# Up projection of a conv-gated FFN: activations as the stationary operand, 512 weight columns moving, and the result turned by transposing DMAs

## The chip, the cores and the metric

The kernel runs on one core of one Trainium2 chip. The metric is the device time of one launch in microseconds (us), the median over runs of the same program. A difference of 0.2%, some 4 us here, is about what such a measurement can tell from no change.

## The reference

Two layers of a bidirectional encoder trunk work on 256 tokens of width 2048 (float32). In each layer a normed copy of `x` goes through one combined input projection, a windowed attention and a spatial gating unit, and an output projection back into `x`. Then comes the feed-forward part, the only part that the change touches in what it computes from what:

```
def rms_norm(x, g):
    y = xf * lax.rsqrt(jnp.mean(xf * xf, axis=-1, keepdims=True) + EPS)
    return y * g

def conv_gated_ffn(h, w_up, conv_w, conv_b, w_down):
    a = depthwise_conv_centred(h @ w_up, conv_w, conv_b)   # 3 taps along the 256 tokens
    g, u = jnp.split(a, 2, axis=-1)                        # 5632 gate, 5632 up columns
    return (jax.nn.silu(g) * u) @ w_down

x = x + conv_gated_ffn(rms_norm(x, norm2_g[l]), w_up[l], conv_w[l], conv_b[l], w_down[l])
```

`w_up` is 2048 x 11264 per layer, `w_down` 5632 x 2048. The depthwise convolution takes, for each channel, the neighbours of a token, so it wants channels on the partitions and tokens along the free dimension.

## The kernel before, in words

**Precision.** Every product of float32 matrices is made of three products in the matmul's 32-bit replicated format `F32R`: each operand is split into a rounded part `hi` and a rest `lo`, and hi·hi, hi·lo and lo·hi are added in PSUM. For weights, ACT makes `hi` from a loaded 1 MB block `raw` (L128), and DVE makes `lo` as `raw - hi` (L112). `raw` has three buffers, `hi` and `lo` four tiles of 128 x 1024 each; one block fills two tiles of each. Activations are split once and kept: 16 tiles `acts[k]` of 128 x 2 x 256, channel k·128.. on the partitions, part 0 rounded, part 1 the rest.

**Two forms of product.** `rows_by_cols` (L161 to L186) serves the input projection, the output projection and the down projection. It holds a 128 x 128 piece of the activations in the array and moves 512 weight columns past it: for each of four k in a block and each half m of the tokens it issues two matmuls with `hi` and one with `lo` as the moving side (L168), 24 matmuls per 1 MB block. The result has tokens on the partitions. `pair` (L222 to L243) and `opening` (L246 to L276) serve the up projection the other way round: a 128 x 128 piece of the weight is held, and the activations move. With `hi` held, both parts of the activation move as 512 columns (L234, in `opening` L275); with `lo` held, only part 0, 256 columns (L240, in `opening` L270). One call of `pair` makes 256 gate channels and the 256 up channels that belong to them in two PSUM tiles: 64 matmuls of 512 columns and 64 of 256, out of 4 MB of weights. The result has channels on the partitions, as the convolution wants it.

**Up stage.** 5632 channels are 44 groups of 128. The first half of the stage makes groups 0 to 23 (12 pairs, the first by `opening`), then the down projection multiplies these; the second half makes groups 24 to 43 (10 pairs), and the down projection takes those. Per layer that is up (12 pairs), down (4 column blocks of 6 weight blocks), up (10 pairs), down (4 column blocks of 5). After each pair, `joined` (L278) adds the two halves of the PSUM tile (ACT copies one, L281; DVE adds, L283), L833 multiplies by the norm factor, which `as_rows` (L363) has spread over the partitions with two PE transposes, `convolved` runs the three taps (ACT L837, DVE L838 and L841), ACT applies SiLU (L855), DVE multiplies gate and up (L857), and `split_plain` splits the product for the down projection (L296, L297).

**Turning rows into columns.** Where a result of `rows_by_cols` is needed with channels on the partitions, the kernel already has a way: ACT copies float32 words apart into their low and high 16-bit halves (L422 in the attention, L575 in `next_rows`), SP issues transposing DMAs on the halves (L429, L582), and ACT puts the halves together again (`together`, L435, and L589 in `next_rows`).

**Order.** A scheduler decides the order on each engine from the order in the program and from priorities; each engine then runs its own list strictly in that order, with waits on the others. `urgent()` raises the priority of what stands in it. `waiting` is a list of steps; `let_in`, called in the middle of each weight block of `rows_by_cols`, issues the steps that stand there, so that the parts of a chain come one weight block after the other. All weight loads and all transposing DMAs are issued by SP and use one queue.

Of the kernel before, what the change touches and what calls it, by code (L numbers as in the profile page):

```python
# [8 lines left out]
F32 = mybir.dt.float32  # L9
# [6 lines left out]
P = 128  # L16
# [11 lines left out]
W = 512  # L28
# [14 lines left out]
def encoder(ctx: ExitStack, tc: tile.TileContext, xT, x, w_in, w_gu, w_o, w_up, w_down, wsT, pcol, prow, rope, out):  # L43
# [4 lines left out]
    slots = pool("slots", 43)  # L48
    rowp = pool("rowp", 4)
# [12 lines left out]
    def row(tag):  # L62
        return rowp.tile([P, W], F32, tag=tag, name=tag)
# [157 lines left out]

    def pair(acts, ws):  # L222
        pss, his, los, later = [mm(), mm()], [], [], []
        for n, w in enumerate(ws):
            hs = []
            for b in range(0, len(acts), UB):
                h, lo = split_weights(w[:, b * UW : (b + UB) * UW], later=later if n else None)
                hs += h
                los += lo if n == 0 else []
            for k in range(len(acts)):  # L230
                for i in range(2):
                    c = k % KB * UW + i * P
                    x1 = acts[k].rearrange("p a b -> p (a b)")
                    nc.tensor.matmul(pss[n][:, i, :], hs[k // KB][:, c : c + P], x1, start=k == 0, stop=False)  # L234
        for n in range(2):
            los = split_later(later) if n else los
            for k in range(len(acts)):
                for i in range(2):
                    c = k % KB * UW + i * P
                    nc.tensor.matmul(  # L240
                        pss[n][:, i, :SEQ], los[k // KB][:, c : c + P], acts[k][:, 0, :], start=False, stop=k == len(acts) - 1
                    )
        return pss  # L243


    def opening(acts, ws, last_step):  # L246
        pss = [mm(), mm()]
        for b0, b1 in ((0, 2), (2, 3), (3, 4)):
            w0, w1 = b0 * KB * UW, b1 * KB * UW
            if b1 - b0 == 2:  # L250
                tiles = [split_weights(w[:, w0:w1]) for w in ws]
            else:
                with urgent():
                    raw = rawp.tile([P, 4 * W], F32, tag="raw", name="raw")
                    for n, w in enumerate(ws):
# [686 lines left out]
```

## Time and profile before

| | us |
|---|---|
| median of 3 runs | 1992.83 (1992.35 to 1993.45) |
| span of the profiled execution, first to last instruction | 1990.9 |
| what lies around the span (median less span) | 1.9 |
| TensorE (PE) busy in the span | 1985.5 |
| VectorE (DVE) busy | 1367.6 |
| ScalarE (ACT) busy | 1134.5 |
| up stage, layer 0: first half, second half | 267.91 to 534.68, 665.27 to 887.31 |
| up stage, layer 1: first half, second half | 1258.22 to 1524.99, 1655.58 to 1878.46 |

The profile is of one execution. A row of a group gives the line, the engine, the operation, output and input names, the count, the busy time of the group, the mean duration of one, and the idle time of the engine ahead of it. Matmuls are pipelined, so the mean duration of one (390 ns) is longer than the distance from one to the next; the distance is read from the chain of work that ended last, which lists stretches of instructions with start, length and count. Busy shares over the whole span mix stages; the tables by stretch of time give them for one stage.

### The profile page before, as it was taken

Reading aid. Unit: us, or ns where it says so; the run is one execution under the profiler, and the core shown is the slowest. Engines: PE = TensorE matmul, PEld = TensorE weight load, DVE = VectorE, ACT = ScalarE, POOL = GpSimd, SP = SyncE. Lnnn points to the kernel's source line nnn. Section 1 sums busy time; section 2 is a strip of 40 time slices with the busy share of each in tenths; the row PEclk is TensorE's granted clock in tenths of the full one; section 3 lists DMA queues with packets and bytes.
Section 4 is the critical chain, followed back from the end, with each engine's and each line's share of the span. In section 5 each row is a group of like instructions: output and inputs, shape, how many; then the busy total and the mean of one; then the engine's idle time right before and its main releaser. Section 6 shows DMA issues by size and latency. Waiting matters only on the chain.

```text
span 1990.9 us, 26332 instructions
## 1 busy us (share of the span) xinstructions
PE 1985.5 (100%) x10292; PEld 1704.8 (86%) x10292; DVE 1367.6 (69%) x1930; ACT 1134.5 (57%) x1514; POOL 23.3 (1%) x25
## 2 busy tenths in 40 slices
PE   9999999999999999999999999999999999999999
PEld 8888888888888888888888888888888888888887
DVE  6778677777754577775566786777777445777753
ACT  6786585556543455556667675855555344555542
POOL 0100000000000000000000000000000000000000
PEclk9999999999999999999999999999999999999999
DMA  9754674455555544556767536745545554455563
GB/s 341 243 161 149 219 222 169 170 208 207 198 191 192 188 170 174 212 207 204 219 205 237 161 142 226 198 169 206 207 180 211 191 192 167 171 208 203 201 212 127
DMA packets 95580, 391.15 MB, mean 196 GB/s; under 512 B 43744, under 2 KB 45024, under 8 KB 50912
## 3 DMA queue, kind: packets, MB, share of 16 engines
q1 hardware_dynamic: 94736, 388.74, 56.6%
q8 instruction: 80, 1.31, 0.3%
q10 hardware_dynamic: 720, 0.73, 0.1%
q14 instruction: 44, 0.36, 0.1%
HBM read 378.43 MB, written 2.10 MB: 191 GB/s over the span
## 4 chain that ended last, share of the span: by engine, by line
PE 97%; ACT 1%; DVE 1%; DMA 1%; issue 0%; SPq 0%; POOL 0%; DVEq 0%; ACTq 0%
PE mm L168 42%; PE mm L234 31%; PE mm L240 16%; PE mm L209 2%; PE mm L275 1%; PE tp L168 1%; PE mm L214 1%; PE mm L270 1%; PE tp L308 0%; PE tp L751 0%; PE tp L310 0%; DVE lo L112 0%; PE tp L309 0%; DMA raw<-in_w_up 0%; ACT hi L128 0%
## 5 line engine op out<-in xcount | busy, mean ns | idle before, releaser
L112 DVE TENSOR_TENSOR lo<-raw,hi 128x1024 fp32r<-128x1024 f32 (+1 forms) x708 | 839.4, 1215 | 417.4 <-ACT hi L128 277.1
L128 ACT ACTIVATE hi<-raw 128x1024 fp32r<-128x1024 f32 (+1 forms) x708 | 730.3, 1050 | 606.8 <-PE mm L168 330.9
L168 PE MATMUL mm<-hi,sl 128*128 128x512 f32 x2480 | 667.6, 390 | 0.1
L234 PE MATMUL mm<-sl,hi 128*128 128x512 f32 x2688 | 617.8, 389 | 0.2 <-ACT hi L128 0.2
L234 PEld LDWEIGHTS mm<-sl,hi 128*128 128x128 f32 x2688 | 501.9, 188 | 103.5 <-ACT hi L128 1.1
L168 PEld LDWEIGHTS mm<-hi,sl 128*128 128x128 f32 x2480 | 464.5, 188 | 97.2 <-DVE sl L289 0.9
L168 PE MATMUL mm<-lo,sl 128*128 128x512 f32 x1240 | 382.6, 390 | 0.0
L240 PEld LDWEIGHTS mm<-sl,lo 128*128 128x128 f32 x2688 | 328.1, 192 | 3.3
L240 PE MATMUL mm<-sl,lo 128*128 128x256 f32 x2688 | 329.1, 283 | 0.0
L168 PEld LDWEIGHTS mm<-lo,sl 128*128 128x128 f32 x1240 | 232.5, 188 | 47.9
L838 DVE SCALAR_TENSOR_TENSOR sc<-ev,pc,sc 128x255 f32<-128x255 f32 x176 | 80.6, 481 | 94.0 <-ACT sc L837 94.0
L281 ACT COPY ev<-mm 128x512 f32<-128x512 f32 x96 | 55.4, 577 | 122.5 <-PE mm L240 114.8
L837 ACT ACTIVATE sc<-ev,pc 128x256 f32<-128x256 f32 x176 | 99.1, 589 | 0.0
L841 DVE SCALAR_TENSOR_TENSOR sc<-ev,pc,sc 128x255 f32<-128x255 f32 x176 | 80.6, 481 | 2.9
L296 ACT ACTIVATE sl<-sl 128x256 fp32r<-128x256 f32 x88 | 31.8, 409 | 72.8 <-DVE sl L857 72.8
L283 DVE TENSOR_TENSOR ev<-mm,ev 128x512 f32<-128x512 f32 x96 | 65.6, 683 | 0.0
L209 PE MATMUL mm<-sl,hi 128*128 128x512 f32 x256 | 61.6, 391 | 0.0
L833 DVE TENSOR_TENSOR ev<-ev,rb 128x512 f32<-128x512 f32 x88 | 60.1, 682 | 0.1
L209 PEld LDWEIGHTS mm<-sl,hi 128*128 128x128 f32 x256 | 47.3, 188 | 9.2
L289 DVE SCALAR_TENSOR_TENSOR sl<-sl,pc 128x256 fp32r<-128x256 f32 x96 | 42.6, 479 | 17.7 <-ACT sl L288 17.6
L297 DVE TENSOR_TENSOR sl<-sl 128x256 fp32r<-128x256 f32 x88 | 33.5, 422 | 19.4 <-ACT sl L296 19.4
L288 ACT ACTIVATE sl<-sl,pc 128x256 fp32r<-128x256 f32 x96 | 43.2, 497 | 1.1 <-DMA sl<-in_xT 0.9
(124 smaller groups left out, 813.2 us busy)
## 6 DMA issues: line engine op xcount, KB each, us to landing
raw<-in_w_up SPq DMA_DIRECT2D x172, 1024.0 KB, 5.2
raw<-in_w_down SPq DMA_DIRECT2D x88, 1024.0 KB, 4.9
raw<-in_w_in SPq DMA_DIRECT2D x38, 1024.0 KB, 5.1
raw<-in_w_o SPq DMA_DIRECT2D x32, 1024.0 KB, 4.9
raw<-in_w_gu SPq DMA_DIRECT2D x16, 1024.0 KB, 4.9
raw<-in_w_up SPq DMA_DIRECT2D x8, 512.0 KB, 4.5
sl<-in_prow SPq DMA_DIRECT2D x12, 256.0 KB, 7.3
raw<-in_w_in SPq DMA_DIRECT2D x8, 256.0 KB, 5.2
```

The source lines that it names most:

```text
L112: nc.vector.tensor_tensor(out=lo, in0=part, in1=hi.bitcast(F32), op=ALU.subtract)
L128: nc.scalar.activation(hi[:, cs], part, AF.Copy)
L168: nc.tensor.matmul(ps[m], acts[kk][:, part % 2, m * P : (m + 1) * P], w, start=first and kk == 0 and part == 0, stop=last and kk == KB - 1 ...
L209: nc.tensor.matmul(ps[:, i, :], tile_of(his, k, i), x1, start=k == 0, stop=False)
L234: nc.tensor.matmul(pss[n][:, i, :], hs[k // KB][:, c : c + P], x1, start=k == 0, stop=False)
L240: nc.tensor.matmul(pss[n][:, i, :SEQ], los[k // KB][:, c : c + P], acts[k][:, 0, :], start=False, stop=k == len(acts) - 1)
L281: nc.scalar.copy(rest, ps[:, :, SEQ:])
L283: nc.vector.tensor_tensor(out=s, in0=ps[:, :, :SEQ], in1=rest, op=ALU.add)
L833: nc.vector.tensor_tensor(out=s, in0=s, in1=r2b2[0], op=ALU.mult)
L837: nc.scalar.activation(t[:, i, :], s[:, i, :], AF.Identity, bias=col(3), scale=col(1))
L838: nc.vector.scalar_tensor_tensor(out=t[:, i, 1:], in0=s[:, i, : SEQ - 1], scalar=col(0), in1=t[:, i, 1:], op0=ALU.mult, op1=ALU.add)
L841: nc.vector.scalar_tensor_tensor(out=t[:, i, : SEQ - 1], in0=s[:, i, 1:], scalar=col(2), in1=t[:, i, : SEQ - 1], op0=ALU.mult, op1=ALU.add)
```

## The change

The up projection goes to `rows_by_cols` as well. `up_rows` multiplies one 1 MB block of `w_up`, now laid out in columns of 512, by the held activations, so four blocks make 512 gate columns (n = 0) or 512 up columns (n = 1), and one step j of the new loop makes both for four groups of 128 channels. That replaces two pairs. `pair` and `opening` go. In the first step of a layer's stage, j = 0, gate and up blocks alternate.

The result then has tokens on the partitions, so `leave` takes it out: for each half m of the tokens ACT copies 128 x 512 out of PSUM and multiplies each row by its norm factor, and ACT copies the words apart into 16-bit halves; `asked` issues four transposing DMAs on SP; three weight blocks after that, in program order, `together` puts the gate's halves into `g`, and in the up part's turn `up_in` puts the up halves together, runs `convolved` on both, SiLU, product and split. `joined`, the multiplication by the norm factor on DVE and the spread of that factor over the partitions are not used in this stage any more. The work buffers `slots` grow from 43 to 58, the separate pool `rowp` goes, and a scratch area for dynamic DMAs is set to 1024.

```
-    slots = pool("slots", 43)
-    rowp = pool("rowp", 4)
+    slots = pool("slots", 58)
...
+    def after(n, step):
+        waiting.append(step if n == 0 else lambda: after(n - 1, step))
...
-        def convolved(ps, ch):
-            s = joined(ps)
-            nc.vector.tensor_tensor(out=s, in0=s, in1=r2b2[0], op=ALU.mult)
+        r2 = inv_rms_rows(ssq, "y")
+
+        def convolved(s, ch):
             t = sc([P, 2, SEQ])
...
+        def up_rows(ps, n, j, b):
+            src = w_up[l, n * (NF // 4) + j, :, b * KB * W : (b + 1) * KB * W]
+            rows_by_cols([ps[:, m, :] for m in range(2)], acts2[b * KB : b * KB + KB], src, b == 0, b == NB - 1)
+
+        def leave(ps, then):
+            halves = []
+            for m in range(2):
+                rows = ev().rearrange("p a b -> p (a b)")
+                with urgent():
+                    nc.scalar.activation(rows, ps[:, m, :], AF.Copy, scale=r2[:, m : m + 1])
+                h = sl([P, 2, 2, SEQ], U16)
+                nc.scalar.copy(h, rows.bitcast(U16).rearrange("p (j n b) -> p j b n", j=2, b=2))
+                halves.append(h)
+            tall = [sl([P, 4, SEQ], U16) for _ in range(2)]
+
+            def asked():
+                for j in range(2):
+                    for m in range(2):
+                        half = halves[m][:, j, :, :].rearrange("p b n -> p (b n)")
+                        nc.sync.dma_start_transpose(tall[j][:, :, m * P : (m + 1) * P], half)
+                after(2, lambda: then(tall))
+
+            waiting.append(asked)
+
+        def gate_and_up(j, ys):
+            g = []
+
+            def gate_in(tall):
+                g.extend(together(t) for t in tall)
+
+            def up_in(tall):
+                for i in range(2):
+                    u = together(tall[i])
+                    f = 4 * j + 2 * i
+                    y = sl([P, 2, SEQ])
+                    nc.scalar.activation(y, convolved(g[i], f), AF.Silu)
+                    t = convolved(u, NF + f)
+                    nc.vector.tensor_tensor(out=y, in0=y, in1=t, op=ALU.mult)
+                    for k in range(2):
+                        ys.append(split_plain(y[:, k, :]))
+
+            if j == 0:
+                pss = [mm(), mm()]
+                for b in range(NB):
+                    for n in range(2):
+                        up_rows(pss[n], n, j, b)
+                        if b == NB - 1:
+                            leave(pss[n], (gate_in, up_in)[n])
+                return
+            for n in range(2):
+                ps = mm()
+                for b in range(NB):
+                    up_rows(ps, n, j, b)
+                leave(ps, (gate_in, up_in)[n])
+
         for f0, f1 in ((0, 24), (24, NF)):
             ys = []
-            for f in range(f0, f1, 2):
-                y = sl([P, 2, SEQ])
...
-                    ps, ps2 = pair(acts2, [w_up[l, f // 2], w_up[l, (NF + f) // 2]])
-                nc.scalar.activation(y, convolved(ps, f), AF.Silu)
...
+            for j in range(f0 // 4, f1 // 4):
+                gate_and_up(j, ys)
...
-        "w_up": blocks(a(w_up), UW),
+        "w_up": blocks(a(w_up), W),
...
-    nc = bacc.Bacc("TRN2", target_bir_lowering=False, num_devices=1)
+    nc = bacc.Bacc("TRN2", target_bir_lowering=False, num_devices=1, dynamic_dma_scratch_size=1024)
```

Because of the lines that go, line numbers shift: L168 of before is L170 in the changed kernel, L128 is L127, L112 is L111, `together` (L435) is L381, the ACT line of `convolved` (L837) is L781, SiLU (L855) is L825 and the ACT line of `split_plain` (L296) is L242.

What moves is seen first on SP, whose list holds both the weight loads and the transposes. Before, in the middle of the first up stage of layer 0, it holds weight loads alone (`raw` is the block's buffer; the numbers only tell buffers apart):

```order
L120 DMA raw_3639<-in_w_up 128x2048
L120 DMA raw_3681<-in_w_up 128x2048
L120 DMA raw_3687<-in_w_up 128x2048
L120 DMA raw_3832<-in_w_up 128x2048
L120 DMA raw_3842<-in_w_up 128x2048
L120 DMA raw_3884<-in_w_up 128x2048
```

In the changed kernel, at the same place, four transposes stand between each four loads (here from the gate columns of one j; the two tiles on the left are `tall`, those on the right the halves of the two token groups):

```order
L119 DMA raw_3211<-in_w_up 128x2048
L119 DMA raw_3260<-in_w_up 128x2048
L809 DMA_TRANSPOSE sl_3102<-sl_3096 128x4x128
L809 DMA_TRANSPOSE sl_3102<-sl_3100 128x4x128
L809 DMA_TRANSPOSE sl_3103<-sl_3096 128x4x128
L809 DMA_TRANSPOSE sl_3103<-sl_3100 128x4x128
L119 DMA raw_3298<-in_w_up 128x2048
L119 DMA raw_3332<-in_w_up 128x2048
L119 DMA raw_3366<-in_w_up 128x2048
L119 DMA raw_3461<-in_w_up 128x2048
```

So a load that stands behind the four is issued only after they are, and they are issued only when ACT has made the halves.

The second place is ACT at the end of layer 0's second up half, where the down projection begins. Before, the tail of the last pair is two copies out of PSUM, four convolution steps, SiLU and two splits (`hi` are the weight tiles, those from `raw_7907` on of the down projection):

```order
L128 ACTIVATE hi_7913<-raw_7907 128x1024
L281 COPY ev_7873<-mm_7703 128x512
L281 COPY ev_7886<-mm_7704 128x512
L128 ACTIVATE hi_7943<-raw_7941 128x1024
L128 ACTIVATE hi_7947<-raw_7941 128x1024
L837 ACTIVATE sc_7878<-ev_7875,pc_92 128x256 x2
L128 ACTIVATE hi_7977<-raw_7975 128x1024
L128 ACTIVATE hi_7981<-raw_7975 128x1024
L128 ACTIVATE hi_8011<-raw_8009 128x1024
L855 ACTIVATE sl_7702<-sc_7878 128x512
L837 ACTIVATE sc_7891<-ev_7888,pc_92 128x256 x2
```

In the changed kernel the copies out of PSUM (L799) and into halves (L801) come first, and `together` (L381), which needs the transposes, stands ahead of weight tiles of the down projection (`hi_7401` and `hi_7405` belong to its fourth block):

```order
L127 ACTIVATE hi_7337<-raw_7331 128x1024
L799 ACTIVATE ev_7281<-mm_7136,yr_2563 128x512
L799 ACTIVATE ev_7285<-mm_7136,yr_2563 128x512
L801 COPY sl_7283<-ev_7281 128x1024
L127 ACTIVATE hi_7367<-raw_7365 128x1024
L801 COPY sl_7287<-ev_7285 128x1024
L127 ACTIVATE hi_7371<-raw_7365 128x1024
L381 COPY sl_7421<-sl_7289 128x2x512
L127 ACTIVATE hi_7401<-raw_7399 128x1024
L825 ACTIVATE sl_7423<-sc_7424 128x512
L781 ACTIVATE sc_7432<-sl_7421,pc_89 128x256
L127 ACTIVATE hi_7405<-raw_7399 128x1024
```

The same sequence of two L799, two L801 and two L381 among the weight tiles stands in ACT's list once per 512 columns through the whole stage. Behind the rows shown follow, still ahead of the fifth block's second weight tile `hi_7489`, three convolution steps, the two splits of the first half and the second L381; behind `hi_7489` two more convolution steps with the SiLU between them, the two tiles of the sixth block, and the last two splits.

More of the change, by code (lines that the diff above doesn't have):

```diff
@@ L60, in sl, with row @@
         return slots.tile(shape, dt, tag="sl", name="sl")
-    def row(tag):
-        return rowp.tile([P, W], F32, tag=tag, name=tag)
+    def row():
+        return sl([P, W])
     def ev():
@@ L219, in unit @@
         return ps
[L222 to L243, printed above, removed]
@@ L469, in attend @@
         for m in range(2):
-            q = row("q")
+            q = row()
             with urgent():
@@ L720, in encoder @@
             for m in range(2):
-                t = row("vn")
+                t = row()
                 with urgent():
```

40 lines of the change are left out of this document (removed).

## The prediction

> **What bounds the kernel now.** I read the page's busy times first, then the chain of work that ended last in order of time, then the busy times by stretch of time, then the groups. The head of the page:
>
> ```profile
> span 1990.9 us, 26332 instructions
> PE 1985.5 (100%) x10292; PEld 1704.8 (86%) x10292; DVE 1367.6 (69%) x1930; ACT 1134.5 (57%) x1514; POOL 23.3 (1%) x25
> PE 97%; ACT 1%; DVE 1%; DMA 1%; issue 0%; SPq 0%; POOL 0%; DVEq 0%; ACTq 0%
> ```
>
> PE is busy for 1985.5 of 1990.9 us, and 97% of the chain lies on it. The time is the number of matmuls by the distance from one to the next; other engines matter where they make PE wait. The distance is read from the chain, where a stretch has a start, a length and a count:
>
> ```profile
> 267.91 3.63 PE mm L275 x16
> ...
> 290.41 14.53 PE mm L234 x64
> 304.94 7.67 PE mm L240 x64
> 312.62 14.53 PE mm L234 x64
> ...
> 534.68 130.59 PE mm L168 x576
> 665.27 14.51 PE mm L234 x64
> ...
> 887.31 176.82 PE mm L168 x780
> ...
> 1258.22 3.63 PE mm L275 x16
> ...
> 1524.99 130.59 PE mm L168 x576
> 1655.58 14.51 PE mm L234 x64
> ...
> 1878.46 81.63 PE mm L168 x360
> ```
>
> In the up stage a matmul of 512 moving columns takes 14.53/64 = 227.0 ns, one of 256 takes 7.67/64 = 119.8 ns, and a pair takes 22.20 us with nothing between. In the down projection, which has the form that the up projection is to get, one of 512 takes 130.59/576 = 226.7 ns. The four up stretches run from 267.91 to 534.68, 665.27 to 887.31, 1258.22 to 1524.99 and 1655.58 to 1878.46: 266.8 + 222.0 + 266.8 + 222.9 = 978.5 us for 44 pairs.
>
> **Matmuls.** A pair moves 64 x 512 + 64 x 256 = 49,152 columns. The new form makes the same 512 output columns of the weight by four blocks of 24 matmuls, 96 x 512 = 49,152 columns: not one column less. What falls away is 32 matmul starts. From the two distances a column costs (227.0 - 119.8)/256 = 0.419 ns, so 12.6 ns of each matmul do not depend on its width; 32 of these are 0.40 us. Directly: 96 x 226.7 ns = 21.76 us against 22.20. For 44 pairs the stage becomes 957.6 us, 20.8 less than 978.5; this holds the two openings (22.5 us each) and 0.8 us of waits in the last stretch.
>
> The Trainium skill would make less of it: "TensorE: Matmul & The Clock Gate", section "Wait — 56ns, not 53.3ns?", gives a warm matmul N/2.4 GHz and about 2.5 ns on top. By that a pair would be 20.80 us, the new form 20.72, and the gain 44 x 32 x 2.5 ns = 3.5 us, an estimate from that page. The rows above disagree with it in both widths (227.0 against 215.8 ns, 119.8 against 109.2), and the sum goes by the rows.
>
> **ACT and DVE in the stage.** The busy times by stretch (length, then PE, PE loads, DVE, ACT, POOL, then clock, DMA share, GB/s), in an up stretch, a down stretch, and a down stretch with transposes in it:
>
> ```profile
> 291.00:535.00 244.00, 244.00 (x1409) 216.37 (x1408) 179.40 (x251) 135.17 (x187) 0.00 (x0) 1.00 0.50 182
> 535.00:665.00 130.00, 130.00 (x575) 107.69 (x574) 70.01 (x70) 55.34 (x58) 0.00 (x0) 1.00 0.60 206
> 887.00:1064.00 177.00, 177.00 (x784) 146.57 (x783) 109.71 (x147) 114.26 (x144) 5.68 (x3) 1.00 0.70 219
> ```
>
> and the groups whose operations go or come:
>
> ```profile
> L281 ACT COPY ev<-mm 128x512 f32<-128x512 f32 x96 | 55.4, 577 | 122.5 <-PE mm L240 114.8 <-PE mm L214 7.7
> L283 DVE TENSOR_TENSOR ev<-mm,ev 128x512 f32<-128x512 f32 x96 | 65.6, 683 | 0.0
> L833 DVE TENSOR_TENSOR ev<-ev,rb 128x512 f32<-128x512 f32 x88 | 60.1, 682 | 0.1
> L723 ACT ACTIVATE vn<-mm,xr 128x512 f32<-128x512 f32 x8 | 5.0, 673 | 0.0
> L575 ACT COPY sl<-xr 128x1024 uint16<-128x1024 uint16 x24 | 23.9, 1045 | 2.9 <-DVE xr L616 2.4
> L589 ACT COPY sl<-sl 128x1024 uint16<-128x1024 uint16 x24 | 32.4, 1350 | 7.2 <-DMA sl<-sl 7.2
> ```
>
> L723 is the copy out of PSUM with a factor per row, L575 the copy into halves, L589 the putting together, all in the sizes of the change. The 244 us hold 11 pairs, so two pairs take 24.6 us of ACT and 32.6 of DVE. Per step j, which replaces two pairs and lasts 2 x 21.76 = 43.5 us, ACT loses four L281 (4 x 55.4/96 = 2.3 us) and gains four of each of the other three (4 x (5.0/8 + 23.9/24 + 32.4/24) = 11.9): 34.2 us, 79% where it was 55%. DVE loses four L283 and four L833 (5.5 us): 27.2 us, 62%. Nothing of this is on PE's path while ACT keeps weight tiles ahead of it, so I cost it at nothing. If that cover goes, every microsecond that ACT lacks in 43.5 is a microsecond of PE, 22 times.
>
> **The transposes.** Rows of before for the same operation, and of what shares the queue:
>
> ```profile
> L582 SPq DMA_TRANSPOSE sl<-sl x48: 1194/1256/2062, 237.2 to 1265.5; - x48
> ...
> DMA to landing us min/median/max: 2.4/4.4/6.8
> ```
>
> ```profile
> raw<-in_w_up SPq DMA_DIRECT2D x172, 1024.0 KB, 5.2
> ```
>
> ```profile
> SPq L120 <- DVE lo L112: 1599.2, 324, 17.4
> ```
>
> ```profile
> ACT hi L128 <- PE mm L168: 330.9, 220, 2.4
> ```
>
> An exit (512 columns, 21.76 us) asks four transposes, 4 x 1.256 = 5.0 us of SP, which spent 1599 us waiting for a free `raw`. A load that stands behind the four goes out up to 5.0 us late. It lands 5.2 us after its issue, and ACT comes to it after the two blocks before it, 2 x 5.44 us: 5.7 us of room. The DMA share was 0.50, is 0.60 in the down form, and 0.70 in the stretch with 16 of the L582 transposes in 177 us; with four in 21.76 us, twice as dense, about 0.80. PE did not wait in that stretch (176.82/780 = 226.7 ns).
>
> The critical place is `together`. In ACT's list stand, after an exit, two copies out of PSUM, two into halves, one more weight tile, then the first `together`, and behind it the weight tiles of the fourth block after the exit. ACT stands there until the transposes land. The second transpose leaves when the last copy into halves is done, so ACT waits the landing time less one weight tile (1.05 us, below): 4.4 - 1.05 = 3.35 us, twice per j, 6.7 us. It has 43.5 - 34.2 = 9.3. That fits, with 2.6 us over; the edge lies at a landing of 9.3/2 + 1.05 = 5.7 us on the mean, between the median and the longest of before.
>
> "VectorE: DVE Perf Modes" of the Trainium skill, section "The three transpose paths", speaks against this road: 1309 ns for one 128 x 128 piece by DMA, 390 ns on TensorE, which it advises where PSUM will do. An exit has 16 such pieces of 16 bits, 20.9 us by that figure, an estimate, against 5.0 us of issue in the row above: the row is of four pieces each.
>
> **The end of a half stage.** The last up exit is followed by its tail while the down projection runs. Rows for the tail:
>
> ```profile
> L128 ACT ACTIVATE hi<-raw 128x1024 fp32r<-128x1024 f32 x700 | 725.2, 1055 | 604.7 <-PE mm L168 330.9 <-issue 184.8 <-DVE lo L112 18.7
> L112 DVE TENSOR_TENSOR lo<-raw,hi 128x1024 fp32r<-128x1024 f32 x700 | 834.0, 1221 | 415.2 <-ACT hi L128 275.0 <-PE mm L240 107.7 <-issue 26.2
> L837 ACT ACTIVATE sc<-ev,pc 128x256 f32<-128x256 f32 x176 | 99.1, 589 | 0.0
> L855 ACT ACTIVATE sl<-sc 128x512 f32<-128x512 f32 x44 | 27.6, 627 | 7.8 <-DVE sc L841 7.5
> L296 ACT ACTIVATE sl<-sl 128x256 fp32r<-128x256 f32 x88 | 31.8, 409 | 72.8 <-DVE sl L857 72.8
> ```
>
> From the last up matmul, in ACT's order: one weight tile 1.05, two copies out 2 x 0.67, copy into halves 1.05, weight tile 1.05, copy 1.05: 5.5 us. The first two transposes land 4.4 later, at 9.9. `together` 1.35, weight tile, SiLU 0.63, convolution step 0.59, weight tile, three steps, weight tile, two splits 0.82, second `together`, weight tile: 20.7. Step, SiLU, step 1.8, two weight tiles 2.1, first split of the second half 0.41: 25.0. PE wants that piece for the third quarter of the group's weight block. In the second half stage that is the fifth block, at 4.5 x 5.44 = 24.5 us: PE is some 0.5 us short, and with the split's rest on DVE about 1.0. In the first half stage the group is the sixth block, 5.4 us later: no wait. Bounds: nothing, if ACT's operations follow each other closer than their mean durations; 3.4 us, if two `lo` of 1.22 us stand between on DVE. I take 1.0 by the nearer rows, twice (two layers): 2.0 us lost.
>
> **Elsewhere.** Work buffers are shared differently, so the scheduler may place attention and gating work otherwise, where ACT and DVE carry 2% of the chain, 40 us. I bound a shift there by a tenth of that, 4 us either way, and take 2 us lost, half of the unfavourable side, as such a wait already stands on PE's path there. The norm factor's two PE transposes per layer go with the openings. The first step's alternation asks the last quarter of the activations 6 blocks after the start instead of 3: nothing lost. Loads of `w_up` keep 1 MB.
>
> The sum: 1990.9 - 20.8 + 2.0 + 2.0 = 1974.1 us of span. Median less span was 1.9 us, so 1976 us, 0.84% less than 1992.8. A difference of 0.2%, 4 us, is about what a measurement of this kernel can tell from no change.
>
> **Rivals.** *The transposes hold ACT (slower).* More transposes share the queue with denser loads, so landings lengthen; ACT stands at the first `together` in strict order while weight tiles wait behind it. For it: the landing's 6.8 us at the longest, ACT at 79%. Against: the median, and the stretch from 887 us without a wait. It decides from a mean of 5.7 us, and the gain is gone at 16.8/22 = 0.76 us per j more, a landing of 6.1. With 6.8 at every exit ACT lacks 2 x 5.75 - 9.3 = 2.2 us per j, 22 times, 48 us: 2024 us. Chance 0.06.
>
> *The tail is long.* Two `lo` per hand-off on DVE at both second half stages: 3.4 instead of 1.0, 6.8 in all: 1981 us. For it: DVE's list is strict too. Chance 0.10, still faster.
>
> *The starts cost nothing (the change does not do what the sum says).* The same columns move before and after, so if a start cost nothing in this stage, a group of 512 columns would take its 22.20 us as before, 231.3 ns for each of 96 matmuls: no gain, 4 us lost, 1997 us, at the edge of no change. Against it: the two widths above, and 226.7 ns over 576 matmuls of the very form that comes. The rule of the skill's TensorE page named above lies close to this case; by it 3.5 us would be gained, an estimate, and the time would be 1993 us. Chance 0.03; another 0.03 for losses of several kinds that together leave no change.
>
> **How the numbers follow.** The forecast, 1976 us, has 0.78. Low end: no tail, and the shift elsewhere in the other direction, 1976 - 2 - 4 = 1970. High end: the long tail, 1981, and landings that pass the edge by 0.07 us each (3 us): 1984. Left out are the slow rival, the rule and the sum of losses, 0.12, and some of the tail. Faster 0.78 + 0.10 = 0.88, the same 0.06, slower 0.06.
>
> **What would show it.** Right: stretches of 96 matmuls of 512 in 21.8 us, a half stage of 12 pairs in 261 us and of 10 in 218; ACT near 80% and DVE near 60% there; transposes landing under 5.7 us; a PE wait of 1 to 3 us in the fifth block of the second down projection and none of note in the first. Wrong: PE waiting for weight tiles (L127) some 15 us after an exit, behind a `together` that waits for the DMA; or a distance other than 226.7 ns in the up stage.

## The result, and the profile after

The changed kernel takes 1971.62 us (median; 1971.57 to 1971.78), the kernel before 1992.84 (1992.35 to 1993.45) beside it on the chip: a ratio of 0.9894, with a 95% interval of 0.9882 to 0.9906. The prediction was 1976.0, with a range of 1970 to 1984. The profiled span went from 1990.9 to 1969.8 us, 21.1 less.

The head of the page of the kernel after:

```profile
span 1969.8 us, 23916 instructions
PE 1963.6 (100%) x8880; PEld 1630.6 (83%) x8880; DVE 1256.4 (64%) x1754; ACT 1316.6 (67%) x1685; POOL 22.6 (1%) x25
```

PE is still the bound. ACT took over work (57% to 67% busy), DVE gave some up (69% to 64%). How far that reaches is seen in the chain of work that ended last, in order of time (start, length, what, count):

```profile
209.41 692.51 PE mm L170 x3055
...
901.96 0.38 DVE sl L243
902.38 152.39 PE mm L170 x671
...
1184.87 696.36 PE mm L170 x3072
...
1881.36 0.43 DVE sl L243
```

Two pieces now hold all four up half stages and the down projections between them. The first has 3055 matmuls: 259 of the layer's output projection, 12 x 96 = 1152 of the up projection, 576 down, 10 x 96 = 960 up, and 108 down. 692.51/3055 = 226.7 ns each, with nothing between. What stops each piece is a split on DVE (L243), for 0.4 us, after 108 of the 480 matmuls of the second down projection, which is in its fifth block of 24.

From the counts come the borders, and so the sum. The first up stage starts at 209.41 + 259 x 0.2267 = 268.1 us (267.9 before). The four half stages hold 2 x (1152 + 960) x 226.7 ns = 957.6 us; they held 978.5. From the second down projection of layer 0 to the first up matmul of layer 1 the kernel takes 370.0 us, from 877.5 to 1247.4, where it took 370.9, from 887.31 to 1258.22. From the last down projection's start to the end it takes 112.9, where it took 112.4. So +0.2 - 20.9 - 0.9 + 0.5 = -21.1 us.

The busy times by stretch (length, then PE, PE loads, DVE, ACT, POOL, then the granted clock of PE, 1.00 for full, the DMA share and GB/s): an up half stage of 12 groups of 512 columns, and one of 10:

```profile
270.00:531.00 261.00, 261.00 (x1153) 216.18 (x1152) 166.80 (x225) 200.25 (x252) 0.69 (x1) 1.00 0.73 219
...
662.00:879.00 217.00, 217.00 (x959) 179.76 (x958) 133.06 (x173) 156.44 (x194) 0.00 (x0) 1.00 0.72 214
```

PE is busy without a break at full clock. The first stretch is six steps j: ACT has 200.25/6 = 33.4 us of work in 43.5 (77%), DVE 27.8 (64%). The group of the joining copy, with what it waited for, and the new transposes (duration of one on the queue, who waited for them, their landing):

```profile
L381 ACT COPY sl<-sl 128x1024 uint16<-128x1024 uint16 x98 | 132.1, 1351 | 119.3 <-DMA sl<-sl 119.2
```

```profile
L809 SPq DMA_TRANSPOSE sl<-sl x176: 1188/1244/2207, 309.0 to 1864.0; - x176
...
  ACT sl L381: 114.2, 44
...
DMA to landing us min/median/max: 2.4/3.5/6.5
```

ACT waits for a transpose once per group of 512 columns, 44 times, 114.2/44 = 2.6 us each. So of the 10.1 us per step j in which ACT is idle, 5.2 go into these waits, and 4.9 are left. In these stretches none of it reaches PE.

### The profile page after: what moved, and what is told of

Its sections match the earlier page's. It is cut to its first block, busy times and chain, and to the rows that moved or that the text cites. A ratio compares the mean times of both kernels' runs of the same rounds, so it can differ in the third digit from the quotient of the medians.

```text
span 1969.8 us, 23916 instructions
## 1 busy us (share of the span) xinstructions
PE 1963.6 (100%) x8880; PEld 1630.6 (83%) x8880; DVE 1256.4 (64%) x1754; ACT 1316.6 (67%) x1685; POOL 22.6 (1%) x25
## 4 chain that ended last, share of the span: by engine, by line
PE 97%; DVE 2%; issue 0%; DMA 0%; SPq 0%; POOL 0%; ACT 0%; DVEq 0%
PE mm L170 91%; PE mm L211 2%; PE tp L170 1%; PE mm L216 1%; DVE lo L111 1%; PE tp L254 0%; PE tp L256 0%; PE tp L255 0%; PE tp L697 0%; PE tp L482 0%; DMA raw<-in_w_in 0%; DVE sl L235 0%; DVE xr L562 0%; SPq L87 0%; DVE sl L265 0%
## 5 line engine op out<-in xcount | busy, mean ns | idle before, releaser
L170 PE MATMUL mm<-hi,sl 128*128 128x512 f32 x5296 | 1418.4, 389 | 0.8 <-DVE sl L243 0.6
L111 DVE TENSOR_TENSOR lo<-raw,hi 128x1024 fp32r<-128x1024 f32 (+1 forms) x708 | 856.5, 1217 | 627.6 <-ACT hi L127 616.7
L170 PEld LDWEIGHTS mm<-hi,sl 128*128 128x128 f32 x5296 | 992.7, 188 | 208.2 <-DVE sl L243 1.5
L127 ACT ACTIVATE hi<-raw 128x1024 fp32r<-128x1024 f32 (+1 forms) x708 | 739.9, 1051 | 461.5 <-PE mm L170 426.0
L170 PE MATMUL mm<-lo,sl 128*128 128x512 f32 x2648 | 816.1, 389 | 0.0
L170 PEld LDWEIGHTS mm<-lo,sl 128*128 128x128 f32 x2648 | 496.9, 188 | 103.1
L381 ACT COPY sl<-sl 128x1024 uint16<-128x1024 uint16 x98 | 132.1, 1351 | 119.3 <-DMA sl<-sl 119.2
L781 ACT ACTIVATE sc<-sl,pc 128x256 f32<-128x256 f32 x176 | 97.0, 588 | 0.0
L801 ACT COPY sl<-ev 128x1024 uint16<-128x1024 uint16 x88 | 89.5, 1037 | 0.0
L782 DVE SCALAR_TENSOR_TENSOR sc<-sl,pc,sc 128x255 f32<-128x255 f32 x176 | 79.1, 479 | 2.6 <-ACT sc L781 2.6
L785 DVE SCALAR_TENSOR_TENSOR sc<-sl,pc,sc 128x255 f32<-128x255 f32 x176 | 79.1, 480 | 1.6
L211 PE MATMUL mm<-sl,hi 128*128 128x512 f32 x256 | 62.0, 391 | 0.0
L211 PEld LDWEIGHTS mm<-sl,hi 128*128 128x128 f32 x256 | 47.3, 188 | 9.3
L799 ACT ACTIVATE ev<-mm,yr 128x512 f32<-128x512 f32 x88 | 54.8, 672 | 0.0
L242 ACT ACTIVATE sl<-sl 128x256 fp32r<-128x256 f32 x88 | 32.1, 410 | 27.9 <-DVE sl L827 27.4
L535 ACT COPY sl<-sl 128x1024 uint16<-128x1024 uint16 x24 | 32.4, 1349 | 6.8 <-DMA sl<-sl 6.8
L216 PE MATMUL mm<-sl,lo 128*128 128x256 f32 x256 | 34.2, 285 | 0.0
L243 DVE TENSOR_TENSOR sl<-sl 128x256 fp32r<-128x256 f32 x88 | 33.3, 419 | 0.0
L216 PEld LDWEIGHTS mm<-sl,lo 128*128 128x128 f32 x256 | 32.4, 191 | 0.6
```

Of the source, the lines that this page charges most:

```text
L111: nc.vector.tensor_tensor(out=lo, in0=part, in1=hi.bitcast(F32), op=ALU.subtract)
L127: nc.scalar.activation(hi[:, cs], part, AF.Copy)
L170: nc.tensor.matmul(ps[m], acts[kk][:, part % 2, m * P : (m + 1) * P], w, start=first and kk == 0 and part == 0, stop=last and kk == KB - 1 ...
L211: nc.tensor.matmul(ps[:, i, :], tile_of(his, k, i), x1, start=k == 0, stop=False)
L216: nc.tensor.matmul(ps[:, i, :SEQ], tile_of(los, k, i), acts[k][:, 0, :], start=False, stop=k == NK - 1)
L381: nc.scalar.copy(words, tall.rearrange("p (b a) n -> p b (a n)", b=2))
```

## The experiments

The main theory: the time is PE's alone, the gain is a cost that each matmul has whatever its width, and everything else of the change is hidden by idle time of ACT. The rivals: the gain comes from somewhere else (other buffers, another order), matmul starts are nearly free, or ACT or the transposing DMAs are a limit already.

### Narrower matmuls: 256 columns

```
for a in range(0, W, step):          # step = W for the first matmul of an output, else 256
    nc.tensor.matmul(ps[m][:, a:a+step], acts[kk][...], w[:, a:a+step], ...)
```

> The changed kernel with every up matmul but the opening one of each output split into two of 256 columns: 190 instead of 96 matmuls per group of 512 columns, the same columns moved. Theory (each matmul costs about 12.6 ns whatever its width): 188 x 119.8 ns + 2 x 226.7 ns = 22.98 us per group where it was 21.76, 44 groups, 54 us more: 1971.6 + 54 = 2025 us, slower than before; a matmul of 256 columns stands 120 ns from the next. Rival (the distance follows the columns, with some 2.5 ns per matmul): 94 x 2.5 ns x 44 = 10 us more, 1982 us. Rival (starts cost nothing): 1972 us.

It took 2026.87 us, ratio to the kernel before 1.0175 (1.0154 to 1.0195). The theory's 2025 holds; the two rivals are 45 us and more away. The same columns, with the same turn and the same buffers, but 94 more matmuls per group, cost 55.3 us: 55.3/(44 x 94) = 13.4 ns per matmul.

### 128 columns

The same edit with 128.

> The same with four matmuls of 128 columns for each one of 512: 378 per group. Theory (fixed 12.6 ns and 0.419 ns per column, down to any width): 66.2 ns each, 376 x 66.2 ns + 2 x 226.7 ns = 25.3 us per group, 3.6 us more, 44 times 157 us: 2129 us. Rival (a narrow matmul can't be shorter than the load of its stationary operand, which stands at 111 ns or more in the trace's short F32 matmuls): 376 x 111 ns = 42 us per group, about 890 us more: 2860 us, and 128 columns cost as much as 256. Rival (starts cost little): 44 x 282 x 2.5 ns = 31 us more, 2003 us.

2880.87 us, 1.446 times the kernel before (1.4433 to 1.449). Here the theory fails and the rival with the load holds. The timelines of PE show it; a row is a run of matmuls with its start, length and count. At 256 columns (8 with `hi` and 4 with `lo` weights make a period), then at 128 (16 and 8):

```profile
402.94 1.12 PE L173 MATMUL mm<-hi,sl 128*128 128x256 f32 x8
...
404.38 1.12 PE L173 MATMUL mm<-hi,sl 128*128 128x256 f32 x8
```

```profile
402.88 1.95 PE L173 MATMUL mm<-hi,sl 128*128 128x128 f32 x16
...
405.56 1.95 PE L173 MATMUL mm<-hi,sl 128*128 128x128 f32 x16
```

From start to start, 1.44 us for 12 matmuls is 120.0 ns, and 2.68 us for 24 is 111.7 ns: half the columns save 8 ns. So 256 columns, the width that the change gave up, stood close above a floor, and two widths alone could not say whether there is a fixed cost per matmul at all.

### Four more widths

```
for a in (0, W - wide):               # not for an output's first and last matmul
    nc.tensor.matmul(ps[m][:, a:a+wide], acts[kk][...], w[:, a:a+wide], ...)
wide = (192, 320, 384, 448)[2 * l + (j >= 6)]
```

> The changed kernel with each up matmul but each output's first and last issued as two of a width that differs by half stage: 192, 320, 384 and 448 columns from the first to the last, the first piece at the left end, the second at the right end of the 512. The pieces leave out or add twice the columns between them, so the up projection is another sum. It tells whether the 12.6 ns are a cost of every matmul, or whether the distance is one rate of 227/512 ns per column that stops falling at some floor close to the 120 ns of 256 columns. Theory (12.6 ns and 0.419 ns per column, with the floor of 111.6 ns that the run with 128 columns gave): 111.6, 146.7, 173.5 and 200.3 ns; 2322 us in all. Rival (0.4434 ns per column above a floor): 112 to 120, 141.9, 170.3 and 198.6 ns; about 2303 us.

One execution took 2388.66 us. The distances, from the timeline of the half stages with 192, 320 and 384 columns:

```profile
351.18 1.05 PE L173 MATMUL mm<-hi,sl 128*128 128x192 f32 x8
...
352.52 1.05 PE L173 MATMUL mm<-hi,sl 128*128 128x192 f32 x8
...
800.94 1.34 PE L173 MATMUL mm<-hi,sl 128*128 128x320 f32 x8
...
802.70 1.34 PE L173 MATMUL mm<-hi,sl 128*128 128x320 f32 x8
...
1500.42 1.55 PE L173 MATMUL mm<-hi,sl 128*128 128x384 f32 x8
...
1502.50 1.55 PE L173 MATMUL mm<-hi,sl 128*128 128x384 f32 x8
```

1.34, 1.76 and 2.08 us for 12 matmuls are 111.7, 146.7 and 173.3 ns. The theory had 111.6, 146.7 and 173.5; the rival with one rate per column had 141.9 and 170.3 for the last two. So the fixed cost is real. The points from 256 to 384 and the 226.7 ns of 512 lie on one line: 13.3 ns and 0.4167 ns per column. Only 448 columns, at 2.43 us for 12 or 202.5 ns, lie 2.5 ns above it; that stays open.

The total missed both numbers, by 67 us for the theory. In the first half stage the scheduler had placed ACT's work in another order, with joining copies behind each other and the weight tiles after them, and PE waited: from 270 to 580 us it was busy for 282.53 of 310 us, at a mean clock of 0.90, which together is most of the miss. The timeline of PE there (a wait ahead of a row stands in brackets), and then the window behind the wait (length, PE busy, clock, DMA share, GB/s):

```profile
360.68 1.24 PE L173 MATMUL mm<-hi,sl 128*128 128x192 f32 x8 [2.63 <-ACT hi L127]
362.33 1.17 PE L173 MATMUL mm<-lo,sl 128*128 128x192 f32 x4 [0.41 <-DVE lo L111]
363.29 1.91 PE L173 MATMUL mm<-hi,sl 128*128 128x192 f32 x8
...
365.85 1.91 PE L173 MATMUL mm<-hi,sl 128*128 128x192 f32 x8
```

```profile
363.30:368.30 5.00, 5.00 (x25) 0.50 0.97 370
```

After waits of 2.63 and 0.41 us the granted clock is 0.50 for 5 us, and 12 matmuls take 2.56 us (363.29 to 365.85) where they took 1.34. So these two waits, 3 us in all, cost PE some 2.5 us more behind them. The waits of 0.4 us in the changed kernel had no such effect (152.39/671 = 227.1 ns behind one). The length of a wait does not decide by itself. In the run with each transpose twice, below, PE waited 2.90 and then 0.29 us (at 344.05 and 345.56) and went on at full clock, and elsewhere waited 1.57 us (at 453.79) and went on, some 1.7 us later, at about half. The windows behind the two:

```profile
346.00:350.00 4.00, 4.00 (x19) 1.00 0.58 178
455.50:458.20 2.70, 2.70 (x8) 0.51 1.03 394
```

What else decides is not shown.

"TensorE: Matmul & The Clock Gate" of the Trainium skill, Part 1 "The HAM clock gate (the "warmup" mystery)", states such a fall to half clock after an idle window of about 3.4 us. The rows agree that the clock falls to half behind an idle stretch, but not on its length: 3 us in two pieces and 1.57 us were enough here, and 2.90 us once was not.

### A smaller stationary operand

```
nc.tensor.matmul(ps[m][:k, a:a+n], acts[kk][:, part % 2, m*P : m*P + k], w[:, a:a+n], ...)
n, k = ((128, 64), (256, 64), (512, 64), (128, 32))[2 * l + (j >= 6)]
```

> Where the floor of 111.6 ns comes from. Up matmuls (but each output's first and last) with a smaller stationary operand, so that part of the output rows is left out: 128 moving columns on 64 stationary, 256 on 64, 512 on 64, and 128 on 32, from the first half stage to the last. Theory (the load of the stationary operand bounds a narrow matmul, and takes less for fewer columns): 128 columns fall from 111.6 to about 66 ns in the first and the last half stage, 256 and 512 columns keep 119.8 and 226.7; 2060 us. Rival (the floor belongs to the moving side, or the load takes the same for any size): 111.6 ns in both, 2425 us.

One execution took 2115.73 us. The timeline with 64 stationary columns: 128 moving, 256 moving in one group and a little later, and 512 moving (rows with `lo` at both ends of four periods of six matmuls):

```profile
465.57 1.12 PE L174 MATMUL mm<-hi,sl 128*64 128x128 f32 x16
...
467.01 1.12 PE L174 MATMUL mm<-hi,sl 128*64 128x128 f32 x16
...
751.35 1.07 PE L174 MATMUL mm<-hi,sl 128*64 128x256 f32 x8
...
752.71 1.07 PE L174 MATMUL mm<-hi,sl 128*64 128x256 f32 x8
...
762.40 1.10 PE L174 MATMUL mm<-hi,sl 128*64 128x256 f32 x8
...
763.80 1.10 PE L174 MATMUL mm<-hi,sl 128*64 128x256 f32 x8
...
1350.34 0.63 PE L174 MATMUL mm<-lo,sl 128*64 128x512 f32 x2
...
1355.86 0.40 PE L174 MATMUL mm<-lo,sl 128*64 128x512 f32 x1
```

128 columns fall from 111.7 to 1.44/24 = 60.0 ns: the floor belongs to the stationary operand, as the theory said. More than it said: 256 columns fall too, from 120.0 to 1.36/12 = 113.3 ns in one group and 1.40/12 = 116.7 in another. Above 0.4167 ns per column that leaves 6.7 ns for 128 moving columns and 6.7 to 10 for 256, where it was 13.3 on 128 stationary columns. But 512 columns on 64 take 5.52/24 = 230.0 ns, which is 16.7 above, and 3.3 more than on 128. So the cost beside the columns changes with the stationary operand, and not by one number; which rule it follows stays open. With 32 stationary columns the distance at 128 moving ones is 60 ns as well. In the half stages with 128 columns PE again waits for ACT, which is why the total lies above the forecast; the windows of the first (from PE's busy time on as in the table of after):

```profile
270.00:590.00 320.00, 277.69 (x4237) 271.58 (x4235) 158.86 (x214) 191.38 (x238) 0.70 (x1) 0.93 0.60 170
```

PE is idle for 42.3 of 320 us, at a mean clock of 0.93.

### The turn on TensorE

```
t = tp([P, 2, SEQ])
nc.tensor.transpose(t[:, i, m*P:(m+1)*P], rows[m][:, cs], ident)    # 8 per group, F32
s = sl([P, 2, SEQ]); nc.scalar.copy(s, t)                           # no halves, no joining copy
```

> The turn by TensorE in place of the transposing DMAs: eight transposes of 128x128 F32 per group into PSUM and a copy out on ACT, no 16-bit halves and no putting together. Theory (PE is full, so whatever PE does is added, while ACT's and SP's share of the turn was hidden): 8 x 44 = 352 transposes at 0.11 to 0.15 us, 39 to 53 us more: 2011 to 2025 us, slower than before although ACT loses some 8 us of work per step j. Rival (the DMA turn holds ACT, or the queue, so that taking it away pays for the transposes): 1972 to 1985 us.

2010.55 us, ratio 1.0093 (1.0076 to 1.011): slower than before the change, at the near end of the theory's 2011 to 2025. From its chain:

```profile
315.05 0.87 PE tp L809 x8
315.92 21.78 PE mm L170 x96
```

Eight transposes take 0.87 us ahead of each group of 21.78, so 44 x 0.87 = 38.3 us; the span grew by 2008.4 - 1969.8 = 38.6. ACT lost 1316.6 - 1189.0 = 127.6 us of work, and nothing of that came back.

### Each transpose twice

```
for to in (dump, tall):      # dump is read by nobody
    ... nc.sync.dma_start_transpose(to[j][:, :, m*P:(m+1)*P], half)
```

> The changed kernel with each group's four transposing DMAs issued twice, first into two buffers that nobody reads: eight per group, 10 us of SP instead of 5 in 21.8, and the needed four land later by 2.5 to 5 us. Theory (the wait for the landing is hidden as long as ACT has spare time: 10 us per step j idle, of which 5.2 are the waits for the landing already): 2 waits x 2.5 to 5 us more per j against 4.9 us that are left: between 0 and 5 us lost per j, 0 to 110 us in all, 1972 to 2080 us, with 1990 as the middle guess; matmuls wait at ACT's weight tiles behind the joining copy. Rival (SP has room and the landing is far from any edge): 1972 us. Rival (queue is the bound: every microsecond of issue is lost): 44 x 5 = 220 us, 2190 us.

2068.68 us, ratio 1.0383 (1.0367 to 1.0398). The joining copy's waits, the landing of all 352 transposes, and the busy times of the whole run:

```profile
ACT sl L382 <- DMA sl<-sl: 270.8, 65, 8.6
```

```profile
DMA to landing us min/median/max: 2.4/2.6/8.6
```

```profile
PE 2003.8 (97%) x8880; PEld 1632.1 (79%) x8880; DVE 1253.3 (61%) x1754; ACT 1316.3 (64%) x1685; POOL 22.7 (1%) x25
```

The needed transposes stand on SP behind four others of 1.257 us each, so they go out at least 5.0 us later, and land 2.6 after that. ACT's waits grow by 270.8 - 119.2 = 151.6 us, 6.9 per step j, where 4.9 were left. That explains 2.0 us per step, 44 in all, of the 97 that were lost. The prediction's formula for its slow rival, with a landing of 5.0 + 2.6 = 7.6 us, gives 2 x 6.55 - 9.3 = 3.8 us per step, 84 in all. PE's busy time divides the loss: it took 2003.8 us for the same 8880 matmuls, 40.2 more than in the changed kernel, and of the 98.0 us that the span grew (2067.8 against 1969.8) the other 57.8 are idle time. So PE's waits lie between the two accounts, and slower matmuls behind them make up the rest. The mean granted clock was 0.992 in this run (1.000 in the changed kernel), which is 0.008 x 2068 = 17 us of the 40.2; what makes the other 23 is not settled. So the cliff is where the prediction saw it and at least as steep: it priced the lost time on ACT, and not the slower matmuls that can follow a wait of PE.

### More work on ACT, ahead of the wait and behind it

```
for _ in range(4):                  # or 8: after the copies into halves, ahead of the transposes
    nc.scalar.copy(junk, rows)      # 128x512, read by nobody
```

> The changed kernel with four more copies of 128x512 on ACT per group, into a tile that nobody reads, right after the copies into halves: eight per step j, about 0.58 us each, 4.6 us. Theory (ACT is idle for 10 us per step of 43.5 us, about half of that in waits for the transposes, so some 4.9 us are spare): nothing or a few us lost, 1972 to 1980 us. Rival (ACT is the hidden bound after the change, and its lists are strict, so the work is paid at once): 22 x 4.6 = 102 us more, 2073 us.

> The same with eight more copies per group: 9.3 us per step j. Theory: 9.3 - 4.9 = 4.4 us lost in each of 22 steps, 97 us, 2068 us; PE waits for weight tiles. Rival (the waits for the transposes shrink as the work moves into them, so all 10 us of idle time are spare): 1972 to 1980 us. Rival (paid in full): 204 us, 2176 us.

```
g.extend(together(t) for t in tall); idle(g[1])    # the same 8 copies, behind the joining copies
```

> The changed kernel with eight more ACT copies of 128x512 per group, as many as the run that cost 8 us, but behind the joining copies of the group in place of ahead of the transposes. Theory (it is the place in ACT's list that decides: ahead of the joining copies such work fills the wait for the transposes, behind them the wait stays and the copies come on top): 9.3 us more per step j against 4.9 that are left beside the waits, some 4 us lost 22 times, 80 to 100 us: 2052 to 2072 us, and the waits of the joining copies for the transposes stay near 100 us in sum. Rival (only ACT's total counts, wherever the work stands): 1980 us as the other run.

Four copies: 1971.52 us, ratio 0.9896 (0.9879 to 0.9914), no difference to the changed kernel. Eight: 1979.93, ratio 0.9939 (0.9922 to 0.9957), 8 us lost and not 97. Eight behind the joining copies: 2046.74, ratio 1.027 (1.0253 to 1.0287), 75 us lost. The rows of the joining copy's waits in the three:

```profile
ACT sl L382 <- DMA sl<-sl: 19.5, 24, 4.1
```

```profile
ACT sl L382 <- DMA sl<-sl: 23.1, 28, 4.2
```

```profile
ACT sl L382 <- DMA sl<-sl: 107.8, 52, 5.2
```

and the first up half stage with eight, early and late:

```profile
270.00:531.00 261.00, 257.52 (x1128) 212.53 (x1128) 161.77 (x218) 239.28 (x329) 0.70 (x1) 0.99 0.71 211
```

```profile
270.00:531.00 261.00, 251.76 (x1081) 204.22 (x1080) 157.26 (x207) 222.00 (x306) 0.69 (x1) 0.98 0.66 202
```

The expectation for the early eight was wrong: it took the waits for the transposes as spent. Work that stands ahead of the joining copy fills them (119.2 us fall to 23.1), and ACT gets to 92% busy there for 8 us lost. The same work behind the joining copy leaves them (107.8), and ACT stands at 85% with nine times the loss. Spare time on an engine that runs its list in order has a place in that list. The two lists are less pure than the edits: the scheduler left about four of the eight early copies ahead of a group's first joining copy and put the others behind it; of the late ones none stands ahead, and in nearly every group all eight stand ahead of the next group's copies into halves, which can make its transposes later too. How much of the 75 us comes from that is not shown.

### The follow-on work one block earlier

```
after(1, lambda: then(tall))        # was after(2, ...), for every group
```

> The changed kernel with the follow-on work of a group (joining, convolution, gating) queued one weight block after the transposes are asked for, not two. Theory (the two waits of 0.4 us in the fifth block of the second down projections come from the tail being late): both go, 0.8 us less, 1970.8 us; in exchange the joining copy stands closer to the transposes, and ACT waits longer for them: if its spare time doesn't hold that, 44 x up to 3 us more. Rival (the tail is set by the landing, not by its place in the list): no difference, 1971.6 us.

1974.08 us (1973.49 to 1974.62), 2.5 more than the changed kernel; ratio 0.9909 (0.9893 to 0.9925). The chain, early in the first up half stage of layer 0 (in layer 1 it has the same row at 1309.65), and its last long piece:

```profile
329.68 0.41 ACT sl L242
...
1315.97 624.99 PE mm L170 x2756
```

The waits of 0.4 us at the tails are gone (the last piece runs through to the last down projection), as the theory has it; but behind the groups of the first step j the joining copy now waits longer for the transposes (over the whole run its waits are shorter, 94.1 us against 119.2), and PE waits three times, 1.8 us in sum, for weight tiles that stand behind it.

### Only the last group's tail earlier

```
leave(ps, (gate_in, up_in)[n], 1 if n and 4 * j + 4 == NF else 2)
```

> The changed kernel with the follow-on work queued one weight block after the transposes, as in the run that did so for every group, but only for the last group of each second half stage. Theory (the 0.4 us waits in the fifth block of the second down projections come from the place of the tail in the lists, and the 2.5 us that the other run lost came from the groups in mid-stage): both waits go and nothing else comes, 0.8 us less than the changed kernel, 1970.8 us. Rival (another wait of the tail takes their place): no difference, 1971.6 us.

1970.59 us (1970.14 to 1970.74), ratio 0.989 (0.9875 to 0.9904). The chain:

```profile
209.75 844.82 PE mm L170 x3727
```

```profile
1184.67 753.47 PE mm L170 x3324
```

Each layer's feed-forward part is now one piece of matmuls without a wait. The span is 1968.9, 0.9 less than the changed kernel's, as expected. The median, 1970.59, is the lowest of the study; a difference of 1.0 us is less than the times alone can tell, and the chain, without the two waits, is what shows it.

### The buffers alone

```
slots = pool("slots", 58)           # kernel before; no rowp, its tiles come from slots; scratch area at 1024
```

> The kernel before with nothing of the change but its sharing of buffers: the four row tiles go into the common pool, which grows from 43 to 58 slots, and the DMA descriptors' scratch shrinks. It tells what of the gain comes from attention and gating being ordered otherwise. Theory (only the up projection's matmuls count; elsewhere the sum moves by about 1 us): 1991.5 to 1993 us, and attention of the second layer about 1 us shorter. Rival (the buffers carry part of the gain): 1980 to 1990 us.

1991.75 us (1990.96 to 1992.71) beside 1992.27, ratio 0.9998 (0.9988 to 1.0007): no difference, as the theory has it. Its chain tells more:

```profile
887.96 176.82 PE mm L167 x780
...
1257.48 3.63 PE mm L274 x16
```

From the second down projection of layer 0 to the first up matmul of layer 1 it takes 369.5 us, where the kernel before takes 370.9: 1.4 us less. The changed kernel, without its 0.4 us wait, takes 369.6. So this small part of the gain seems to belong to the sharing of buffers. It rests on one trace of each kernel, and the two times, 0.5 us apart, are too close to confirm it.

## Why the prediction was right, step by step

**Matmuls.** Forecast 957.6 us for the four half stages, 20.8 less; measured 957.6. The reason held too: each matmul has a cost beside its columns. The two widths of the page had put it at 12.6 ns; four of the seven widths tried (256, 320, 384 and 512) put it at 13.3, with 0.4167 ns per column. That two widths were enough was in part luck: the narrower one stood 8 ns above the floor. Every matmul here has its own load of the stationary operand (8880 of each in the changed kernel, 13016 of each with 256 columns), so the runs do not tell a cost of the matmul from a cost of its load. The first distance was read a touch low from 7.67 us (119.8 ns where the timeline has 120.0), without effect on the sum, which went by measured distances.

The Trainium skill's N/2.4 GHz in "TensorE: Matmul & The Clock Gate", section "Wait — 56ns, not 53.3ns?", agrees with the 0.4167 ns per column. Its 2.5 ns on top do not agree with these F32R matmuls: 13.3 ns on 128 stationary columns, and 6.7 to 16.7 on 64. The gain hung on that term, and the rival drawn from it is ruled out by the runs with 256, 320 and 384 columns.

**ACT and DVE.** Forecast 34.2 and 27.2 us per step j, measured 33.4 and 27.8, hidden as forecast. The runs with more copies show how firmly: 4.6 us per step more in front of the transposes cost nothing.

**Transposes.** Forecast: a landing of 4.4 us, a wait of 3.35 per group, a DMA share of 0.80. Measured: 3.5, 2.6, 0.73. The critical place was the right one (ACT at the first joining copy), with more room than forecast. The edge at a mean landing of 5.7 us was not reached (median 3.5, longest 6.5); the run with doubled transposes went past it and lost 97 us. The prediction took ACT's room as its idle time less the waits. That is the room behind the joining copies (75 us lost with 9.3 us more there, 97 by that account), not ahead of them.

**The end of a half stage.** Forecast 1.0 us twice, in the fifth block of the second down projection and nowhere else. Measured 0.38 and 0.43 at that very place. That the waits come from the tail is shown by the edit of the last group's tail, which takes both away. The size was over by more than half, and the late engine was another: the prediction had ACT's first split some 0.5 us behind PE's need. The rows ahead of the first wait, of ACT and then of DVE:

```profile
900.89 0.73 ACT L242 ACTIVATE sl<-sl 128x256 fp32r<-128x256 f32 x2 [1.06 <-DVE sl L827]
...
900.78 1.22 DVE L111 TENSOR_TENSOR lo<-raw,hi 128x1024 fp32r<-128x1024 f32 x1
901.91 0.75 DVE L243 TENSOR_TENSOR sl<-sl 128x256 fp32r<-128x256 f32 x2
```

ACT's first split, one of two in the row at some 0.41 us each, is done at 901.3, some 23.8 us after the last up matmul (877.5) where the forecast had 25.0, and 0.6 us before PE stops at 901.92. DVE's part of the split stands in DVE's list behind a weight tile `lo` of 1.22 us, and starts only at 901.96. So the hand-off on DVE, which the prediction had priced only in its long tail, made the wait: one `lo` stood there, and ACT's lead took up part of it.

**Elsewhere.** Forecast 2.0 us lost, measured 0.2 lost in layer 0 and 1.3 gained in layer 1. The sign was wrong: taking the unfavourable side of an unknown had no row behind it. The run with the buffers alone points to the sharing of buffers as the gain's cause.

These two terms, 4.0 us forecast as lost against some 0.2 gained, make up the miss of 4.3 us in the span (1974.1 against 1969.8).

**The turn.** The Trainium skill's advice in "VectorE: DVE Perf Modes", section "Rules for kernel authors", to turn on TensorE where a result in PSUM will do and by DMA otherwise, does not hold in this kernel, where TensorE is the bound: its way costs 38.9 us, the DMA's shows no wait on PE but the 0.4 us of the tails. The price of a 128 x 128 F32 transpose in that run is 0.87/8 = 0.11 us.

## What to carry to other kernels

Where PE is busy throughout, count its matmuls as well as their columns: here each cost 13.3 ns beyond its columns, and one of 128 or 192 columns on a full stationary operand took 111.7 ns. (By these two figures the floor ends at some 235 columns, an estimate.) Work that left PE for an engine with idle time was free here, even though that engine and the DMAs do far more of it, up to the edge that the doubled transposes passed; so a turn that is cheaper by itself can still be the dearer one. Ask where in an engine's list its idle time lies: work placed ahead of a wait fills it, work behind it comes on top.

## What the runs showed of the hardware that was not expected

- An F32R matmul's distance has a floor that belongs to its stationary operand: 111.7 ns with 128 columns, for 128 and 192 moving columns alike. With 64 or 32 columns 128 moving ones took 60.0 ns.
- The part of the distance beside 0.4167 ns per moving column changes with the stationary operand: 13.3 ns with 128 columns; with 64 it was 6.7 ns at 128 moving columns, 6.7 to 10 at 256, and 16.7 at 512 (230.0 ns).
- Behind waits of 2.63 and 0.41 us the granted clock of PE was 0.50 for 5 us, so they cost nearly twice their length; behind one of 1.57 us it was 0.51 for 2.7 us, behind one of 2.90 us it was 1.00. Waits of 0.4 us cost only themselves.
- With the four transposing DMAs asked twice, the landing of a single one was 2.6 us in the median (3.5 before) and 8.6 at the longest (6.5); what grows is the time until the needed ones are issued, some 1.25 us of SP for each ahead of them.
